# A list scheduler that books VectorE's and GpSimd's SBUF port as one resource, with matmul and ScalarE prices taken from a trace

## The chip, the core and the metric

The kernel runs on one core of one Trainium2 chip. The metric is the device time of one execution in microseconds. Five engines matter: TensorE (PE in the rows; its weight loads are PEld), VectorE (DVE), ScalarE (ACT), GpSimd (POOL) and SyncE (SP), which here only issues DMAs. Each engine works through its own instructions strictly in the order in which they were issued, and waits on semaphores where an operand or a buffer is not ready.

## What is computed

Two transformer stacks of two layers each follow one another on x, a float32 array of 512 tokens by 1024 features.

```python
def first_block(x, ...):
    for layer in range(2):
        x = x + 0.5 * rmsnorm(swiglu(rmsnorm(x, g[0]), gate, up, down), g[1])     # 1024 -> 2816 -> 1024
        x = x + rmsnorm(token_mixer(rmsnorm(x, g[2]), ...), g[3])                 # 16 heads, three kinds of attention
        x = x + 0.5 * rmsnorm(swiglu(rmsnorm(x, g[4]), gate, up, down), g[5])
    return x

def second_block(x, ...):
    for l in range(2):
        mix = concat(hgrn2_mixer(...), nsa_mixer(...)) @ w_out                    # a gated scan and sparse attention
        x = layer_norm(ALPHA * x + mix)
        x = layer_norm(ALPHA * x + (silu(x @ gate) * (x @ up)) @ down)
    return x
```

## The kernel before

Features lie on the 128 partitions and tokens along a partition, so x is eight tiles of 128x512 (in the rows `x_70`, `x_72`, and so on). Each projection is split in precision: a float32 weight block lands by DMA in a tile `raw`, and `weights` makes two tiles `ws` from it, hi = the block rounded to fp32r and lo = raw - hi. Activations are split in the same way into `h`, `m` or `gu`. `accum` then issues three fp32r matmuls for each block of 128 features (hi by hi, hi by lo, lo by hi) into a PSUM tile `mm`. So for 128x512 of weights there is one copy (VectorE or ScalarE) and one subtraction (VectorE or GpSimd), and TensorE gets twelve matmuls out of them.

Between the projections stand the norms. `rsqrt` is a chain of twelve tiny VectorE instructions on 128x2 tiles named `sm`: three `tensor_scalar`, then three rounds of one `tensor_tensor` and two `scalar_tensor_tensor`. `spread` transposes its result over the partitions (tile `nb`). `tail` and `post` scale the projected `y` by it (`tc<-y,nb`), add the product to x (`x<-x,tc`), and the next norm squares, adds (`tc<-tc`) and splits (`h<-tc,h`). Each half of 256 tokens goes through this by itself, so that TensorE can work on one half while the other is normed.

The order of all of this is not written by hand. A `Recorder` takes down every operation, with its operands, and `order` runs a list scheduler over them. `price` gives each operation a duration on each engine that may run it, `LAT` gives the delay to a consumer on another engine, and `attempt` runs forward in time: whenever an engine is idle it takes the ready operation of the smallest priority. The operations recorded with `nc.either` stand in the ready lists of two engines, and the one that is idle first takes them: copies and scalings go to VectorE or ScalarE, two-input operations (`tensor_tensor`) to VectorE or GpSimd. `holds` may keep an engine idle for something more urgent that comes soon. `backward` computes new priorities from the schedule found; twelve rounds are made and the shortest schedule by the prices is issued. `issue` (line 665) emits every instruction, so nearly all rows of the trace carry L665.

The prices that matter here, before: an fp32r matmul of n columns costs n/2.4 + 2.5 ns; ScalarE costs n/1.2 plus 52 or 94 ns; a GpSimd `tensor_tensor` 90 + 2.22 n ns; a VectorE `tensor_tensor` 70 + n/0.96 ns. VectorE and GpSimd are priced as independent of each other.

Of the kernel before, what the change touches and what calls it, by code (L numbers as in the profile page):

```python
# [26 lines left out]


class Buf:
    """A logical tile. Its slot and its Tile tile come when the order of instructions is known."""  # L30

    def __init__(self, parts, cols, dt, tag, name, dram=None):
        self.parts, self.cols, self.dt, self.tag, self.name, self.dram = parts, cols, dt, tag, name, dram
# [15 lines left out]


class V:
    """A view of a logical tile: partitions, and an access pattern over a partition's elements."""

    def __init__(self, buf, dt, p0, np_, off, dims, pstep=None, raw=None):
        self.buf, self.dt, self.p0, self.np, self.off, self.dims, self.raw = buf, dt, p0, np_, off, dims, raw
# [121 lines left out]

class Op:
    __slots__ = ("eng", "meth", "args", "kw", "outs", "ins", "deps", "users", "left", "cost", "lat", "tail", "ready",
                 "idx", "bufs", "func", "end", "start", "busy", "prices", "forms")  # L180

    def __init__(self, idx, eng, meth, args, kw):
        self.idx, self.eng, self.meth, self.args, self.kw = idx, eng, meth, args, kw
        vs = [x for x in args if isinstance(x, V)]
        outs = []
        ins = []
        for i, x in enumerate(args):
            if isinstance(x, V):
                (outs if i == 0 or i == 3 and meth == "pair" else ins).append(x)
        for k, x in kw.items():  # L190
            if isinstance(x, V):
                (outs if k == "accum_out" else ins).append(x)
        self.outs, self.ins = outs, ins
        self.deps, self.users = {}, []
        self.bufs = list({id(v.buf): v.buf for v in outs + ins}.values())
        self.func = args[2] if meth == "activation" and args[2] in SETS else None
        self.prices = {}
        self.forms = {}
        if meth == "copy":
            forms = {"vector": ("tensor_copy", args, kw), "scalar": ("activation", args + (AF.Copy,), kw)}  # L200
        elif meth == "scale":
            out, src, by = args
            forms = {"vector": ("tensor_scalar", (out, src, by, None), {"op0": OP.mult}),
                     "scalar": ("activation", (out, src, AF.Copy), {"scale": by})}
        else:
            forms = {e: (meth, args, kw) for e in (("vector", "gpsimd") if eng == "either" else (eng,))}
        for e in forms:
            self.eng = e
            self.meth, self.args, self.kw = forms[e]
            self.price()  # L210
            self.prices[e] = self.cost
        self.forms = forms
        self.choose(next(iter(forms)))

    def choose(self, eng):
        self.eng, self.cost = eng, self.prices[eng]
# [2 lines left out]
    def price(self):  # L219
        m = self.meth  # L220
        out = self.outs[0] if self.outs else None
        n = out.count() if out is not None else 0
        vs = self.ins + self.outs
        psum = any(v.buf.tag in PSUM for v in vs)
        if self.eng == "tensor":
            lhs = self.ins[0]
            load = lhs.count() / 1.2
            if lhs.dt == F32R:
                self.busy = n / 2.4
                self.cost = max(n / 2.4 + 2.5, load)  # L230
            elif m == "transpose":
                self.busy = self.cost = 107
            elif m == "pair":
                self.busy = 4 * n / 2.4
                self.cost = self.busy + 110
            else:
                self.busy = 4 * n / 2.4
                self.cost = max(self.busy + 2, 2 * load if n > 8 or n == 1 else load)
        elif self.eng == "sync":
            self.cost = max(475, vs[0].count() * vs[0].np / 90.0)  # L240
        elif self.eng == "scalar":
            self.cost = (52 if psum else 94) + n / 1.2 + (187 if "accum_out" in self.kw or isinstance(self.kw.get("bias"), V) else 0)
        elif self.eng == "gpsimd":
            self.cost = 90 + {"memset": 1.0, "tensor_copy": 3.5}.get(m, 2.22) * n
        else:
            ptr = any(v.count() == 1 for v in self.ins[1:])
            if m in ("tensor_copy", "tensor_scalar", "memset") and not psum:
                self.cost = 65 + n / 1.92 + (64 if ptr else 0)
            elif m == "reciprocal":
                self.cost = 65 + 8 * n / 0.96  # L250
            elif m == "tensor_tensor_reduce" or m == "tensor_reduce":
                self.cost = 75 + self.ins[0].count() / 0.96
            else:
                self.cost = 70 + n / 0.96 + (60 if psum and m == "scalar_tensor_tensor" else 0)
# [8 lines left out]
PSUM = ("mm", "at", "pv", "nb", "ah")  # L263
# [10 lines left out]


class Recorder:
    """Records instructions on logical tiles, orders them by a list scheduler, and issues them in that order."""

    def __init__(self, nc, tc, ctx, plan):
        self.bass_nc, self.tc, self.ctx, self.plan = nc, tc, ctx, plan  # L280
# [105 lines left out]
        return out  # L386

    def backward(self):
        """Schedules the reversed instructions, those that ended last first; the starts in forward time."""
        ops = self.ops  # L390
        engines = ("tensor", "scalar", "vector", "gpsimd", "sync")
        ready = {e: [] for e in engines}
        idle = {e: True for e in engines}
        left = [len(op.users) for op in ops]
        freed = [()] * len(ops)
        for b in self.bufs:
            if b.slot is not None and b.prior is not None and b.opener is not None:
                freed[b.opener] += tuple(b.prior.members)
                for i in b.prior.members:
                    left[i] += 1  # L400
        at = [0.0] * len(ops)
        late = [0.0] * len(ops)
        events = []
        for op in ops:
            if left[op.idx] == 0:
                heapq.heappush(ready[op.eng], (-op.end, op.idx))
        now, done = 0.0, 0
        while done < len(ops):
            for e in engines:
                if idle[e] and ready[e]:  # L410
                    i = heapq.heappop(ready[e])[1]
                    idle[e] = False
                    heapq.heappush(events, (now + ops[i].cost, 0, i))
            now, kind, i = heapq.heappop(events)
            op = ops[i]
            if kind:
                heapq.heappush(ready[op.eng], (-op.end, i))
                continue
            idle[op.eng] = True
            done += 1  # L420
            late[i] = -now
            for d in op.deps:
                left[d] -= 1
                at[d] = max(at[d], now + LAT[ops[d].eng][op.eng])
                if left[d] == 0:
                    heapq.heappush(events, (at[d], 1, d))
            for d in freed[i]:
                left[d] -= 1
                at[d] = max(at[d], now + (2000 if ops[d].eng == "sync" else 180))
                if left[d] == 0:  # L430
                    heapq.heappush(events, (at[d], 1, d))
        return late

    def attempt(self, prio):
# [20 lines left out]
        engines = ("tensor", "scalar", "vector", "gpsimd", "sync")  # L455
# [54 lines left out]
        def free_at(op, e):  # L510
            t = 0.0
            for b in op.bufs:
                if b.bank:
                    for g, end in b.last.items():
                        if g != e:
                            t = max(t, end + LAT[g][e])
            return t

        def holds(op, e, p):
# [5 lines left out]
                    return True  # L525
            return False

        def fits(op):
            return op.func is None or table in SETS[op.func]

        table = None
        now, done, total, out = 0.0, 0, len(ops), []
        loads = {}
        busy, window, cold = {}, 1, True
        while done < total:
            for e in engines:
                put_off = []
                while idle[e] and ready[e]:
                    op = None
                    while ready[e] and op is None:  # L540
                        p, i = heapq.heappop(ready[e])
                        if ops[i].start is not None:
                            continue
                        t = free_at(ops[i], e)
                        if t > now:
                            push(t, "ready", ops[i])
                            continue
                        if e == "scalar" and not fits(ops[i]):
# [8 lines left out]
                                    break  # L557
                            if op is not None:
                                break
                        if e in HOLD and holds(ops[i], e, p):  # L560
                            put_off.append((p, i))
                            op = None
                            break
# [22 lines left out]
                    if not fits(op):  # L586
                        cost += 1300
                        table = SETS[op.func][0]
                        loads[op.idx] = table
                    op.start, op.end = now, now + cost  # L590
                    for b in op.bufs:
                        if b.bank:
                            b.last[e] = op.end
# [75 lines left out]

SET_SLACK = 4000  # L670
HOLD = ('gpsimd', 'scalar', 'vector')
HOLD_A = 0.3
HOLD_B = 0.5
ROUNDS = 12
# [1179 lines left out]
```

## Time and profile before

| | |
|---|---|
| time, median of 3 runs | 3787.7 us (3786.96 to 3789.73) |
| span of the profiled execution, first to last instruction | 3776.2 us |
| TensorE busy | 3631.1 us (96%) |
| VectorE busy | 2241.1 us (59%) |
| ScalarE busy | 1699.6 us (45%) |
| GpSimd busy | 1078.0 us (29%) |
| mean granted TensorE clock | 0.978 of 2.4 GHz |

The profiled execution is told by its span alone; the timed runs lie 10.8 to 13.5 us above it, which is what stands before the first and behind the last instruction. Busy times are the union of an engine's instructions. An engine that waits on another engine's port inside an instruction counts as busy.

### The profile page before, as it was taken

How to read it: one execution, taken by the hardware profiler on the slowest of the kernel's cores; microseconds unless marked ns; L12 is line 12 of the kernel's file. 1: busy time of each engine (PE TensorE's matmuls, PEld its weight loads, DVE VectorE, ACT ScalarE, POOL GpSimd, SP SyncE). 2: the span in 40 equal slices, each digit the busy share in tenths (PEclk: the TensorE clock that was granted, in tenths of full speed). 3: DMA queues.
4: the chain of work that ended last, by engine and by line, in shares of the span. 5: the costliest groups of instructions: out<-in, count | busy, mean ns of one | idle time of the engine just before them, and what ended most of it. 6: DMA issues, size and time to landing. Idle time of an engine off the chain costs nothing.

```text
span 3776.2 us, 56593 instructions
## 1 busy us (share of the span) xinstructions
PE 3631.1 (96%) x20836; PEld 3016.9 (80%) x20836; DVE 2241.1 (59%) x4611; ACT 1699.6 (45%) x3550; POOL 1078.0 (29%) x999
## 2 busy tenths in 40 slices
PE   8999899999999999899899999999999999999998
PEld 7878877778898889767788897668888977678888
DVE  7443787764367545886844384677333766674335
ACT  5333456543344334565433354465332555654324
POOL 3220422443224211522633042334111333232112
PEclk9999999999999999999999999899999999999999
DMA  5224422232353224312322452013323531123234
GB/s 165 95 93 133 157 81 76 96 112 95 95 150 124 95 92 144 130 59 74 125 98 93 118 173 93 29 32 123 112 95 102 172 98 51 40 90 129 95 90 139
DMA packets 121622, 393.08 MB, mean 104 GB/s; under 512 B 14813, under 2 KB 20102, under 8 KB 121345
## 3 DMA queue, kind: packets, MB, share of 16 engines
q1 hardware_dynamic: 121344, 389.47, 32.6%
q8 instruction: 164, 2.69, 0.3%
q14 instruction: 114, 0.93, 0.1%
HBM read 384.65 MB, written 4.77 MB: 103 GB/s over the span
## 4 chain that ended last, share of the span: by engine, by line
PE 47%; DVE 6%; issue 1%; ACT 1%; POOL 0%; DMA 0%; ACTq 0%; DVEq 0%; POOLq 0%; SPq 0%
PE mm L665 38%; PE at L665 4%; PE ah L665 2%; PE pv L662 2%; DVE ws L665 1%; PE ah L662 1%; DVE sm L665 1%; DVE tc L665 1%; DVE hw L665 1%; DVE h L665 1%; DVE x L665 0%; PE nb L665 0%; ACT ws L665 0%; POOL ws L665 0%; ACT L659 0%
## 5 line engine op out<-in xcount | busy, mean ns | idle before, releaser
L665 PE MATMUL mm<-h,ws 128*128 128x512 f32 (+1 forms) x9792 | 2102.3, 362 | 53.9 <-DVE ws L665 16.9
L665 PEld LDWEIGHTS mm<-h,ws 128*128 128x128 f32 x9792 | 1645.8, 192 | 357.8 <-issue 25.1
L665 ACT ACTIVATE ws<-raw 128x512 fp32r<-128x512 f32 (+1 forms) x1283 | 782.0, 616 | 1417.8 <-PE mm L665 1370.8
L665 POOL TENSOR_TENSOR ws<-raw,ws 128x512 fp32r<-128x512 f32 (+1 forms) x506 | 654.5, 1295 | 2061.6 <-ACT ws L665 1592.3
L665 DVE TENSOR_TENSOR ws<-raw,ws 128x512 fp32r<-128x512 f32 (+2 forms) x926 | 682.3, 741 | 798.6 <-ACT ws L665 732.1
L665 PE MATMUL mm<-gu,ws 128*128 128x256 f32 (+1 forms) x4752 | 813.0, 323 | 11.9 <-DVE ws L665 7.3
L665 PEld LDWEIGHTS mm<-gu,ws 128*128 128x128 f32 x4752 | 692.2, 191 | 90.5 <-DVE ws L665 12.9
L665 DVE TENSOR_TENSOR te<-te,mm 128x256 f32<-128x256 f32 (+1 forms) x228 | 98.8, 460 | 279.9 <-PE mm L665 275.2
L665 PE MATMUL mm<-ws,h 128*128 128x256 f32 (+1 forms) x1344 | 254.9, 303 | 1.7 <-DVE sm L665 0.7
L665 PE MATMUL mm<-m,ws 128*128 128x256 f32 (+1 forms) x1248 | 218.3, 321 | 7.5 <-DVE ws L665 7.2
L665 PEld LDWEIGHTS mm<-ws,h 128*128 128x128 f32 x1344 | 203.2, 195 | 14.7 <-issue 6.3
L665 PEld LDWEIGHTS mm<-m,ws 128*128 128x128 f32 x1248 | 175.6, 195 | 32.3 <-issue 12.4
L665 ACT ACTIVATE row<-row,sm 128x512 f32<-128x512 f32 (+2 forms) x267 | 148.3, 572 | 58.2 <-DVE sm L665 57.2
L665 ACT ACTIVATE gu<-te 128x256 fp32r<-128x256 f32 (+1 forms) x210 | 89.5, 452 | 129.8 <-DVE te L665 118.4
L665 DVE TENSOR_TENSOR te<-te,rt 128x256 f32<-128x256 f32 x157 | 119.4, 792 | 0.5
L665 DVE CAST ws<-raw 128x512 fp32r<-128x512 f32 x149 | 97.7, 656 | 33.2 <-PE mm L665 27.7
L665 DVE TENSOR_TENSOR te<-mm,rt 128x256 f32<-128x256 f32 x176 | 67.8, 419 | 81.7 <-PE mm L665 80.4
L665 POOL TENSOR_TENSOR hw<-hw 128x256 f32<-128x256 f32 x106 | 88.7, 846 | 92.9 <-ACT hw L665 80.0
L665 PE MATMUL at<-c_ident,row 128*128 128x128 f32 x528 | 114.4, 286 | 0.4 <-DVE sm L665 0.3
L665 DVE TENSOR_TENSOR gu<-te,gu 128x256 fp32r<-128x256 f32 (+1 forms) x159 | 94.2, 611 | 30.3 <-ACT gu L665 26.0
L665 DVE CUSTOM_DVE_ANT_0 row<-at,T 128x128 f32<-128x128 f32 (+1 forms) x180 | 88.8, 509 | 25.6 <-PE at L665 23.6
L665 ACT ACTIVATE hw<-hw 128x256 f32<-128x256 f32 (+2 forms) x181 | 75.5, 456 | 55.1 <-DVE hw L665 28.1
(249 smaller groups left out, 3429.7 us busy)
## 6 DMA issues: line engine op xcount, KB each, us to landing
raw<-in_wg_dram SPq DMA_DIRECT2D x156, 512.0 KB, 3.3
raw<-in_wu_dram SPq DMA_DIRECT2D x156, 512.0 KB, 3.2
raw<-in_wd_dram SPq DMA_DIRECT2D x144, 512.0 KB, 3.5
raw<-in_wd_dram SPq DMA_DIRECT2D x72, 384.0 KB, 3.2
raw<-in_wout_dram SPq DMA_DIRECT2D x52, 512.0 KB, 3.3
raw<-in_w_f_dram SPq DMA_DIRECT2D x52, 512.0 KB, 3.4
raw<-in_win_f_dram SPq DMA_DIRECT2D x44, 512.0 KB, 3.3
raw<-in_win_v_dram SPq DMA_DIRECT2D x20, 512.0 KB, 3.2
```

The source lines that it names most:

```text
L662: nc.tensor.matmul(*args[0:3], **kw)
L665: r = getattr(getattr(nc, op.eng), op.meth)(*args, **kw)
```

## The change

`port` (new) marks, for each engine, the operations that use the shared port: on GpSimd all that read a tile from SBUF, on VectorE those with two inputs of more than one element in SBUF, and copies or `tensor_scalar` from SBUF to SBUF. In `attempt`, such an operation cannot start on one of the two engines while the other holds the port (`held`). `late` (new) lets GpSimd take a two-input operation only when VectorE is busy and would finish it later, counting what is ready ahead of it on VectorE. Three prices change.

```diff
+        self.ports = {e: self.port(e) for e in forms}
...
+    def port(self, e):
+
+        wide = [v for v in self.ins if v.count() > 1]
+        if e == "gpsimd":
+            return bool(wide)
+        if e != "vector":
+            return False
+        near = [v for v in wide if v.buf.tag not in PSUM]
+        if len(near) == 2:
+            return True
+        return (len(near) == len(wide) == 1 and self.outs[0].buf.tag not in PSUM
+                and self.forms[e][0] in ("tensor_copy", "tensor_scalar"))
...
-                self.cost = max(n / 2.4 + 2.5, load)
+                self.cost = max(n / 2.4 + 13, load)
...
-            self.cost = (52 if psum else 94) + n / 1.2 + (187 if "accum_out" in self.kw or isinstance(self.kw.get("bias"), V) else 0)
+            self.cost = (62 if psum else 106) + n / 1.2 + (187 if "accum_out" in self.kw or isinstance(self.kw.get("bias"), V) else 0)
...
-            self.cost = 90 + {"memset": 1.0, "tensor_copy": 3.5}.get(m, 2.22) * n
+            self.cost = 130 + {"memset": 1.0, "tensor_copy": 3.5}.get(m, 2.2) * n
...
+        def late(op):
+            if idle["vector"]:
+                return False
+            t = until["vector"]
+            n = sum(ops[x[1]].prices["vector"] for x in ready["vector"] if ops[x[1]].start is None and x[0] < prio[op.idx])
+            return t + n + op.prices["vector"] > now + op.prices["gpsimd"] * POOL_W
...
+                        if ops[i].ports[e]:
+                            t = max(t, held["vector" if e == "gpsimd" else "gpsimd"])
                         if t > now:
                             push(t, "ready", ops[i])
                             continue
...
+                        if e == "gpsimd" and "vector" in ops[i].prices and not late(ops[i]):
+                            put_off.append((p, i))
+                            op = None
+                            break
...
+                    until[e] = op.end
+                    if op.ports[e]:
+                        held[e] = op.end
...
+POOL_W = 1.0
```

The operations recorded are the same in both kernels; which engine issues them and in what order is not. In the built programs GpSimd's `tensor_tensor` instructions go from 961 to 253 (of those with 512 elements from 506 to 149), and VectorE's from 2711 to 3419: 708 of them move. VectorE's copies, casts and `tensor_scalar` go from 835 to 692, and ScalarE's activations from 3274 to 3417: 143 of them move.

Two places show it, both at the end of the first layer's attention block, where its norm and the start of the second feed-forward block stand close together. First GpSimd's order there. Before, from the splits of the gate weights (`ws<-raw,ws`) over the additions to x to the splits of the next `h`:

```order
L665 TENSOR_TENSOR ws<-raw,ws 128x512 x5
L665 TENSOR_TENSOR te<-te,rt 128x256
L665 TENSOR_TENSOR gu<-te,gu 128x256
L665 TENSOR_TENSOR x_72<-x_72,tc 128x256
L665 TENSOR_TENSOR x_74<-x_74,tc 128x256
L665 TENSOR_TENSOR x_78<-x_78,tc 128x256
L665 TENSOR_TENSOR ws<-raw,ws 128x512
L665 TENSOR_TENSOR x_88<-x_88,tc 128x256
L665 TENSOR_TENSOR ws<-raw,ws 128x512
L665 TENSOR_TENSOR h<-tc,h 128x256
L665 TENSOR_TENSOR ws<-raw,ws 128x512
L665 TENSOR_TENSOR h<-tc,h 128x256
```

And GpSimd's whole order over the same place now, from the splits of the attention output `m` to an addition to x of the next norm:

```order
L697 TENSOR_TENSOR m<-y,m 128x512 x4
L697 TENSOR_TENSOR ws<-raw,ws 128x512 x4
L697 TENSOR_TENSOR x_84<-x_84,tc 128x256
L697 TENSOR_TENSOR ws<-raw,ws 128x512 x2
L697 TENSOR_TENSOR te<-te,rt 128x256
L697 TENSOR_TENSOR ws<-raw,ws 128x512 x2
L697 TENSOR_TENSOR ws<-raw,ws 128x256
L697 TENSOR_TENSOR x_72<-x_72,tc 128x256
```

Of the four additions to x, the two splits of `h` and all but a few of the weight splits nothing is left on GpSimd here. They stand on VectorE, whose order at the norm of the second half of the tokens was this, from the end of the `rsqrt` chain:

```order
L665 SCALAR_TENSOR_TENSOR sm<-sm 128x2
L665 TENSOR_TENSOR te<-te,mm 128x256
L665 TENSOR_TENSOR ws<-raw,ws 128x512
L665 TENSOR_TENSOR tc<-y,nb 128x256 x2
L665 TENSOR_TENSOR x_70<-x_70,tc 128x256
L665 TENSOR_TENSOR tc<-y,nb 128x256 x4
L665 TENSOR_TENSOR x_76<-x_76,tc 128x256
L665 TENSOR_TENSOR x_84<-x_84,tc 128x256
L665 TENSOR_TENSOR tc<-y,nb 128x256 x2
L665 TENSOR_SCALAR tc<-x_72,c_gains 128x256
L665 TENSOR_TENSOR x_94<-x_94,tc 128x256
```

and is this now:

```order
L697 SCALAR_TENSOR_TENSOR sm<-sm 128x2 x2
L697 TENSOR_TENSOR ws<-raw,ws 128x512
L697 CAST ws<-raw 128x512
L697 TENSOR_TENSOR tc<-y,nb 128x256 x4
L697 TENSOR_TENSOR x_70<-x_70,tc 128x256
L697 TENSOR_TENSOR x_72<-x_72,tc 128x256
L697 TENSOR_TENSOR x_74<-x_74,tc 128x256
L697 TENSOR_TENSOR x_84<-x_84,tc 128x256
L697 TENSOR_TENSOR tc<-y,nb 128x256 x2
L697 TENSOR_TENSOR x_78<-x_78,tc 128x256
L697 TENSOR_TENSOR tc<-y,nb 128x256
L697 TENSOR_TENSOR x_76<-x_76,tc 128x256
```

Before, VectorE made four of the eight additions to x and GpSimd the other four; now all eight stand on VectorE (the last two a few rows on).

## Rows read from the trace of the kernel before

**Rows 1.** Page: busy us, share, instructions; VectorE's busy tenths in 40 slices.

```profile
PE 3631.1 (96%) x20836; PEld 3016.9 (80%) x20836; DVE 2241.1 (59%) x4611; ACT 1699.6 (45%) x3550; POOL 1078.0 (29%) x999
...
DVE  7443787764367545886844384677333766674335
```

**Rows 2.** Span and mean granted TensorE clock.

```profile
core 0: 3776.2 us, clock 0.978
```

**Rows 3.** Windows: length; busy us (count) of PE, PEld, DVE, ACT, POOL; clock; DMA.

```profile
300.00:400.00 100.00, 100.00 (x571) 83.02 (x570) 33.03 (x54) 37.29 (x71) 3.42 (x4) 0.98 0.52 156
400.00:500.00 100.00, 85.46 (x635) 80.23 (x634) 90.57 (x192) 50.53 (x114) 50.68 (x46) 0.97 0.44 142
700.00:800.00 100.00, 84.63 (x606) 80.32 (x605) 84.86 (x172) 49.97 (x105) 55.69 (x51) 0.91 0.39 126
...
800.00:1000.00 200.00, 199.21 (x863) 161.76 (x863) 89.56 (x159) 72.18 (x141) 63.54 (x53) 1.00 0.29 95
```

**Rows 4.** TensorE's waits: total us, times, longest.

```profile
PE mm L665 <- DVE ws L665: 31.3, 35, 5.2
PE nb L665 <- DVE sm L665: 27.9, 17, 3.8
PE mm L665 <- ACT ws L665: 16.6, 5, 12.0
PE mm L665 <- POOL ws L665: 8.0, 11, 1.5
PE nb L665 <- DVE tc L665: 6.7, 10, 1.6
PE mm L665 <- DVE te L665: 5.7, 5, 3.8
PE nb L665 <- POOL tc L665: 5.0, 4, 2.8
```

**Rows 5.** Timeline around 741 us: start, length, instruction.

```profile
740.92 1.28 POOL L665 TENSOR_TENSOR ws<-raw,ws 128x512 fp32r<-128x512 f32 x1 [2.68 <-ACT ws L665]
740.93 1.29 DVE L665 TENSOR_TENSOR sm<-sm 128x2 f32<-128x2 f32 x1
```

**Rows 6.** VectorE's groups, 300 to 400 us: busy us, mean ns, idle before.

```profile
L665 DVE TENSOR_TENSOR ws<-raw,ws 128x512 fp32r<-128x512 f32 x36 | 24.8, 692 | 53.9 <-ACT ws L665 50.7 <-PE mm L665 3.0
...
L665 DVE CAST ws<-raw 128x512 fp32r<-128x512 f32 x1 | 0.4, 428 | 3.4 <-PE mm L665 3.4
L665 DVE TENSOR_SCALAR sm<-sm 128x2 int32<-128x2 int32 x2 | 0.3, 170 | 0.1
L665 DVE TENSOR_TENSOR sm<-sm 128x2 f32<-128x2 f32 x1 | 0.2, 161 | 0.0
```

**Rows 7.** VectorE's groups, 700 to 800 us.

```profile
L665 DVE TENSOR_TENSOR ws<-raw,ws 128x512 fp32r<-128x512 f32 x23 | 20.1, 882 | 5.7 <-ACT ws L665 3.0 <-PE mm L665 2.7
L665 DVE TENSOR_TENSOR h<-tc,h 128x256 fp32r<-128x256 f32 x13 | 8.2, 642 | 0.1
L665 DVE TENSOR_TENSOR x<-x,tc 128x256 f32<-128x256 f32 x10 | 7.9, 816 | 0.0
L665 DVE TENSOR_TENSOR tc<-tc 128x256 f32<-128x256 f32 x9 | 6.6, 731 | 0.2
...
L665 DVE TENSOR_TENSOR sm<-sm 128x2 f32<-128x2 f32 x12 | 5.0, 415 | 0.3
L665 DVE TENSOR_SCALAR sm<-sm 128x2 int32<-128x2 int32 x8 | 4.9, 618 | 0.2
L665 DVE SCALAR_TENSOR_TENSOR sm<-sm 128x2 f32<-128x2 f32 x24 | 4.9, 205 | 0.7
...
L665 DVE TENSOR_TENSOR te<-te,mm 128x256 f32<-128x256 f32 x8 | 3.3, 417 | 2.7 <-PE mm L665 2.7
```

**Rows 8.** GpSimd's largest group, 700 to 800 us.

```profile
L665 POOL TENSOR_TENSOR ws<-raw,ws 128x512 fp32r<-128x512 f32 x26 | 34.5, 1329 | 27.3 <-ACT ws L665 22.6 <-PE mm L665 3.0 <-issue 0.8
```

**Rows 9.** A VectorE group with one input in PSUM, whole span.

```profile
L665 DVE TENSOR_TENSOR te<-te,mm 128x512 f32<-128x512 f32 x36 | 24.8, 688 | 92.8 <-PE mm L665 92.8
```

More of the change, by code (lines that the diff above doesn't have):

```diff
@@ L179 @@
     __slots__ = ("eng", "meth", "args", "kw", "outs", "ins", "deps", "users", "left", "cost", "lat", "tail", "ready",
-                 "idx", "bufs", "func", "end", "start", "busy", "prices", "forms")
+                 "idx", "bufs", "func", "end", "start", "busy", "prices", "forms", "ports")
     def __init__(self, idx, eng, meth, args, kw):
@@ L531, in attempt @@
         table = None
+        held = {"vector": 0.0, "gpsimd": 0.0}
+        until = dict.fromkeys(engines, 0.0)
         now, done, total, out = 0.0, 0, len(ops), []
```

## Prediction, made before the changed kernel was run

> **What bounds the kernel now.** I read the busy times first. TensorE is busy 3631.1 of 3776.2 us, VectorE 59% and GpSimd 29% [rows 1, 2]. TensorE's idle time is so 3776.2 - 3631.1 = 145 us. Its granted clock averages 0.978; the clock has two levels, 1.2 and 2.4 GHz, so the low level costs at most 0.022 x 3776 = 83 us of full-speed work [rows 2]. Then the windows, which tell where this happens. Between 800 and 1000 us TensorE works through 863 matmuls of 512 columns in 200 us and waits for nothing: 231.7 ns for one, at a granted clock of 1.00. Between 700 and 800 us, where a norm closes the attention block and the next feed-forward block starts, it is busy 84.6 of 100 us at a clock of 0.91, while VectorE is busy 84.9 and GpSimd 55.7; 400 to 500 us looks alike (90.6 and 50.7) [rows 3]. So the kernel is bound by TensorE in the long projections and by VectorE with GpSimd in the stretches around the norms. TensorE's own waits say the same: the largest are for `ws` and the `rsqrt` chain `sm`, both from VectorE, and 8.0 + 5.0 = 13.0 us are for GpSimd [rows 4].
>
> **What the port does in this trace.** A `tensor_tensor` on 128x2 that takes 161 ns where GpSimd is nearly idle [rows 6] took 1.29 us when it started 10 ns behind a GpSimd instruction of 1.28 us [rows 5]: it was held for the whole of it. From the means of 700 to 800 us against undisturbed ones (692 ns for `ws`, 161 and 170 ns for `sm`; 417 ns for 128x256, from `te<-te,mm`, which has an input in PSUM) [rows 6, 7], the time held is: `ws` 23 x (882 - 692) = 4.4 us, `h` 13 x 225 = 2.9, `x` 10 x 399 = 4.0, `tc<-tc` 9 x 314 = 2.8, `sm` 12 x 254 + 8 x 448 = 6.6; together 20.7 us beside 55.7 us of GpSimd's work [rows 3], or 0.37 us for each. Over GpSimd's 1078 us [rows 1] that makes some 400 us of VectorE's 2241, an estimate.
>
> **The change part by part.** *708 `tensor_tensor` move from GpSimd to VectorE.* 357 have 512 elements, the others mostly 256: 357 x 0.692 + 351 x 0.417 = 393 us of new VectorE work. GpSimd keeps 253 of 961, so if the held time falls with its count, 400 x 708 / 961 = 295 us come back. *143 copies and scalings move to ScalarE*, which relieves VectorE of 143 x 0.43 = 61 us at most [rows 6]; I take 55, since many have 256 elements. Sum for VectorE: 2241 + 393 - 295 - 55 = 2284 us. For 700 to 800 us: 51 GpSimd instructions, 26 of them `ws` [rows 3, 8]; 74% of them cost 19 x 0.692 + 19 x 0.417 = 21 us, 20.7 x 0.74 = 15 us come back and about 2 us of copies leave, so 84.9 becomes 89 us. **In throughput the move is a wash, slightly against the change.** What is left is latency, and the plan.
>
> *Latency of GpSimd's share.* A `ws` comes after 692 instead of 1329 ns [rows 6, 8]. TensorE's 13.0 us of waits for GpSimd should about halve: -6 us. *Latency of the `rsqrt` chain.* Of its 14.8 us in rows 7 (three `sm` groups) 6.6 are held time, 45%. TensorE waits 27.9 us for it [rows 4]; 27.9 x 0.45 x 0.74 = -9 us. *Other waits for VectorE* (31.3 + 6.7 + 5.7 [rows 4]): a VectorE that is 5% fuller delays them by 5%, +2 us. *ScalarE* gets 143 of 1699.6 us' worth of instructions more, about 4%; its 16.6 us of TensorE's waits [rows 1, 4] grow by 1 us. *Clock.* TensorE's idle time falls by 12 of 145 us, 8%, and with it, I assume, the share at the low level: 83 x 0.08 = -7 us.
>
> *The prices and the new order.* All 20,836 matmuls stand in another order, and no row of before prices that. The matmul's price of 512 columns goes from 215.8 to 226.3 ns where the row shows 231.7 [rows 3], so the plan now counts on a slower TensorE, nearer to what it does. What a nearer plan can give lies between nothing gained and a loss of the size of the waits that the order itself causes. Upwards I bound it by half of the seven waits shown (half of 101 us) plus the clock in proportion (50 x 83/145 = 29): -80 us. Downwards by an order whose waits grow by a fifth, 20 us. I take -16, near the small end, because the waits shown are of a few us after a chain of data, which an order can only fill with other work, not shorten.
>
> The Trainium skill, "TensorE: Matmul & The Clock Gate", section "Back-to-back issue gap", gives the distance of warm matmuls as N/2.4 GHz plus about 2.5 ns, which is the price before. The trace disagrees: 231.7 ns against 215.8 for 512 columns. By that rule the new price is an error, the order term is its upper bound of +20 instead of -16, and the sum +1 us, 3789; the rows leave that 0.04, which is held in rival 2.
>
> Sum: -6 - 9 + 2 + 1 - 7 - 16 = -35 us. The span of 3776.2 us would be 3741; the median of the timed runs lies 11.5 us above the span, and I keep that: 3787.7 - 35 = **3752 us**. Less than 0.2% (7.6 us) can't be told from no change with this kernel.
>
> **The rivals.** *1. VectorE becomes the bound at the norms (slower).* GpSimd's work beside a VectorE instruction with an input in PSUM was free: `te<-te,mm` of 512 elements shows 688 ns in the mean of 36, no longer than an undisturbed one [rows 6, 9]. This free overlap is given up. The point that decides is how much held time comes back: if only half of the 15 us does, VectorE needs 84.9 + 21 - 7.5 - 2 = 96 of 100 us between 700 and 800, and by the same ratio over 100 between 400 and 500. Added VectorE work then lies on the path: 11 us for each such stretch. Five of the 40 slices of the span show VectorE at eight tenths or more [rows 1]; half of 11 us on each, and the low clock that goes with idle time (83/145 of it), give 5 x 5.5 x 1.57 = +43 us, less the 15 us of latency gained: 3816 us. Against it: 74% fewer instructions that can hold the port, each booked against VectorE, should give back more than half. The Trainium skill, "SBUF — State Buffer", section "Who interferes with whom", says that a VectorE instruction with at most one SBUF input outside its two-port modes does not contend with GpSimd. The trace agrees: 688 ns [rows 9]. By that rule this overlap was indeed free before, and what is left of it on GpSimd is now decided by who would end sooner alone.
>
> *2. No change.* The two engines did the same work through one port before and do it after; 2284 against 2241 us is the same. Then only the latency terms are left and the order takes them back: -15 + 8 = 3781 us, or within 0.2%. For it speaks that TensorE is busy 96% [rows 1]. The Trainium skill, "Trace Analysis", section "Optimizing Scalar/DVE Operations", says that shifting work between GpSimd and VectorE might not help since they share a port; by that rule the shift back need not help either, which is this case.
>
> *3. Much faster.* The plan was wrong by far (engines thought independent, TensorE 7% too fast by 215.8 to 231.7), and an order made with right prices removes half of the waits and of the low clock: -80 us from the order instead of -16, 3688 us.
>
> *4. The change doesn't do what it says:* GpSimd's remaining instructions still overlap with VectorE's, because nothing on the chip enforces the plan. That is inside rival 1 (held time doesn't come back) and needs no chance of its own.
>
> **How the numbers follow.** My forecast (3710 to 3775) gets 0.42, rival 3 (below 3710) 0.18, rival 2 (3775 to 3795) 0.18, rival 1 (above 3795) 0.22. The predicted time is the forecast's. The range to leave out no more than 2 in 10: from 3695, which leaves out the far half of rival 3 (0.08), to 3815, which leaves out the far half of rival 1 (0.11), 0.19 in all. The forecast and rival 3 alone reach from 3688 to 3775. Faster by over 0.2% means below 3780: 0.42 + 0.18 and a little of rival 2, 0.62. Slower, above 3795: 0.22 and a little of rival 2, 0.24. Between: 0.14.
>
> **What would show it.** Right: mean durations of VectorE's `sm`, `x<-x,tc` and `h<-tc,h` at 700 to 800 us fall towards 161, 417 and 417 ns; GpSimd's busy time is near 300 us and VectorE's within 80 us of 2284; TensorE's waits for `sm` and for GpSimd fall by a third or more; the mean clock rises from 0.978. The latency step is wrong if the durations fall and the waits don't. The throughput step is wrong if VectorE's busy time goes over 2400 us, with idle time of TensorE before `ws` from VectorE above 31.3 us. The order term is wrong if stretches without any wait of before, 800 to 1000 us for one, get longer, or if TensorE's idle time falls by far more than 30 us. The whole is wrong if TensorE's busy time itself grows by tens of us at an equal clock.

## The result and the profile after

| | before | after |
|---|---|---|
| median of 4 runs each | 3787.3 us (3786.67 to 3789.73) | 3675.1 us (3665.83 to 3678.68) |
| ratio | | 0.9699 [0.9684, 0.9714] |

The kernel is 112 us faster. The forecast of 3752 us had the sign and missed the size by a factor of three, and the time lies below the range. The profiled execution after took 3672.3 us, 1.8 us above its span. So the 10.8 to 13.5 us by which the timed runs before lie above the profiled span are mostly a difference between executions, not time before the first and behind the last instruction; the two spans differ by 106 us, the medians by 112.

The page of the kernel after, busy us, share and instructions of each engine, then VectorE's busy tenths in 40 slices, answers to [rows 1]; its span and granted clock to [rows 2]:

```profile
PE 3592.3 (98%) x20836; PEld 2990.6 (81%) x20836; DVE 2205.6 (60%) x5176; ACT 1750.3 (48%) x3690; POOL 289.4 (8%) x291
...
DVE  6443788755366545986844385677333767774336
```

```profile
core 0: 3670.5 us, clock 0.985
```

GpSimd lost 789 us of busy time and VectorE, which took over its work, lost 36 as well. TensorE's idle time went from 145.1 to 3670.5 - 3592.3 = 78.2 us, which is 67 us; the other 39 of the 106 us that the span lost are TensorE's own busy time, at the same number of matmuls and a clock of 0.985 instead of 0.978.

Three stretches of after in windows, with the columns of [rows 3]. Work ends earlier now, so 680 to 780 us holds what 700 to 800 us held:

```profile
300.00:400.00 100.00, 100.00 (x571) 81.84 (x571) 33.87 (x60) 38.23 (x71) 1.49 (x2) 1.00 0.54 159
...
680.00:780.00 100.00, 89.58 (x647) 84.73 (x646) 78.64 (x208) 56.47 (x126) 7.08 (x6) 0.95 0.41 138
800.00:1000.00 200.00, 200.00 (x866) 162.17 (x865) 90.95 (x197) 69.73 (x134) 3.33 (x3) 1.00 0.29 95
```

The long projections are as they were (866 instead of 863 matmuls in 200 us). At the norm VectorE does more instructions (208 instead of 172) in less time (78.6 instead of 84.9 us), TensorE is busy 89.6 instead of 84.6, and the clock rose from 0.91 to 0.95. Why VectorE got faster stands in its groups of 680 to 780 us, which answer to [rows 7] (busy us, mean ns of one, idle before):

```profile
L697 DVE TENSOR_TENSOR ws<-raw,ws 128x512 fp32r<-128x512 f32 x48 | 32.2, 686 | 5.1 <-ACT ws L697 4.2 <-PE mm L697 0.6
L697 DVE TENSOR_TENSOR x<-x,tc 128x256 f32<-128x256 f32 x15 | 7.7, 555 | 0.0
L697 DVE TENSOR_TENSOR h<-tc,h 128x256 fp32r<-128x256 f32 x16 | 6.9, 450 | 0.2 <-ACT h L697 0.2
...
L697 DVE SCALAR_TENSOR_TENSOR sm<-sm 128x2 f32<-128x2 f32 x24 | 3.8, 160 | 0.7
L697 DVE TENSOR_TENSOR te<-te,mm 128x256 f32<-128x256 f32 x8 | 3.3, 418 | 5.4 <-PE mm L697 5.4
L697 DVE TENSOR_TENSOR sm<-sm 128x2 f32<-128x2 f32 x12 | 1.9, 161 | 0.4
L697 DVE TENSOR_SCALAR sm<-sm 128x2 int32<-128x2 int32 x8 | 1.3, 169 | 0.2
```

`ws` fell from 882 to 686 ns, the three `sm` groups from 415, 618 and 205 to 161, 169 and 160 ns: the first three of these four at their undisturbed values of [rows 6], the last at the 158 ns that it takes in experiment 3, where GpSimd is silent. `x<-x,tc` is at 555 ns, still above the 417 that it takes there. `te<-te,mm`, with an input in PSUM, is at 418 ns where it was at 417.

TensorE's largest waits after, against [rows 4] (total us, times, longest):

```profile
PE mm L697 <- DVE ws L697: 17.6, 17, 5.0
PE nb L697 <- DVE tc L697: 16.9, 8, 11.6
PE mm L697 <- ACT ws L697: 10.1, 9, 4.0
PE nb L697 <- DVE sm L697: 6.4, 6, 2.4
...
PE mm L697 <- POOL ws L697: 0.8, 2, 0.5
```

The wait for the `rsqrt` chain fell from 27.9 to 6.4 us, that for `ws` from VectorE from 31.3 to 17.6, those for GpSimd nearly to nothing. One wait grew: for VectorE's `tc`, 6.7 to 16.9 us, 11.6 of it in one place.

### The profile page after: what moved, and what is told of

The parts are those of the page before. It is cut to its first block, busy times and chain, and to the rows that moved or that the text cites. A ratio compares the mean times of both kernels' runs of the same rounds, so it can differ in the third digit from the quotient of the medians.

```text
span 3670.5 us, 56063 instructions
## 1 busy us (share of the span) xinstructions
PE 3592.3 (98%) x20836; PEld 2990.6 (81%) x20836; DVE 2205.6 (60%) x5176; ACT 1750.3 (48%) x3690; POOL 289.4 (8%) x291
## 4 chain that ended last, share of the span: by engine, by line
PE 92%; DVE 5%; ACT 1%; issue 1%; DMA 1%; SPq 0%; POOL 0%; ACTq 0%; DVEq 0%
PE mm L697 78%; PE at L697 6%; PE pv L694 2%; PE ah L697 2%; PE nb L697 2%; PE ah L694 1%; DVE tc L697 1%; DVE ws L697 1%; DVE x L697 1%; DVE sm L697 1%; DVE h L697 0%; ACT tc L697 0%; DMA cw<-in_cw_dram 0%; SPq L697 0%; ACT ws L697 0%
## 5 line engine op out<-in xcount | busy, mean ns | idle before, releaser
L697 ACT ACTIVATE ws<-raw 128x512 fp32r<-128x512 f32 (+2 forms) x1355 | 822.8, 616 | 1365.5 <-PE mm L697 1329.8
L697 DVE TENSOR_TENSOR ws<-raw,ws 128x512 fp32r<-128x512 f32 (+1 forms) x1286 | 880.5, 690 | 780.7 <-ACT ws L697 662.4
L697 POOL TENSOR_TENSOR ws<-raw,ws 128x512 fp32r<-128x512 f32 (+1 forms) x146 | 184.6, 1265 | 2338.5 <-PE mm L697 1206.2
L697 ACT ACTIVATE gu<-te 128x256 fp32r<-128x256 f32 (+1 forms) x226 | 100.4, 452 | 141.6 <-DVE te L697 140.4
L697 DVE TENSOR_TENSOR gu<-te,gu 128x256 fp32r<-128x256 f32 (+1 forms) x228 | 104.0, 463 | 14.5 <-ACT gu L697 2.5
L697 PE MATMUL at<-NK,NQ 128*128 128x256 f32 (+5 forms) x256 | 89.1, 395 | 0.9 <-DVE sm L697 0.9
L697 PEld LDWEIGHTS at<-c_ident,row 128*128 128x128 f32 x528 | 67.9, 142 | 19.5 <-issue 6.0
L697 DVE TENSOR_TENSOR te<-te,rt 128x256 f32<-128x256 f32 x174 | 83.5, 490 | 0.0
```

The source lines that it names most:

```text
L697: r = getattr(getattr(nc, op.eng), op.meth)(*args, **kw)
```

## The experiments

**Theory A, the held port:** GpSimd's instructions stop VectorE's, and fewer of them mean shorter chains at the norms; this acts in any order. **Theory B, the plan:** what counts is that the planner's numbers became truer (rival 3's mechanism), the new matmul price above all. A third reading lies between: GpSimd's own results were late, since it is slow, and holding VectorE mattered little. Every kernel was timed in three rounds beside the kernel before, whose median was 3783 to 3788 us on these chips. "Held" below is my own sum over VectorE's groups: their time, less their count at the means that the same groups have in `e3_old_order_no_pool`, where GpSimd is silent. By it 389 us were held before and 71 after.

**1. The prices alone** (`e1_prices_only`), in the kernel before:

```diff
-                self.cost = max(n / 2.4 + 2.5, load)
+                self.cost = max(n / 2.4 + 13, load)
```

with the two other prices of the change.

> The kernel before with only the three new prices (matmul, ScalarE, GpSimd); no port, no late rule. Theory A (GpSimd held VectorE's instructions, and that delay was what TensorE waited for): the engines keep their shares, GpSimd stays near 1078 us busy and some 400 us of VectorE's time stays held, so 3780 us, give or take 10. Theory B (the plan counted on a TensorE 7% too fast, and the order made with the right price brings the gain): most of the 112 us, 3700 to 3730 us.

Measured: 3785.8 us, ratio 1.0008 [0.9997, 1.0018]; held 407 us. No change.

**2. The port and the `late` rule with the three old prices** (`e2_port_only`).

> The changed kernel with the three old prices: port and late rule alone. Theory A: nearly the whole gain, 3675 to 3700 us, GpSimd under 350 us busy. Theory B: little, 3755 to 3785 us.

Measured: 3662.5 us, 0.9677 [0.9663, 0.9692]; held 52 us. The whole gain is there without the prices.

**3. The order of before, GpSimd's work on VectorE** (`e3_old_order_no_pool`). In `issue`, each two-input operation that the plan gave to GpSimd, 961 in all, is issued at its place on VectorE:

```diff
+                if op.eng == "gpsimd" and "vector" in op.prices:
+                    op.choose("vector")
```

> The order of the kernel before, untouched on every engine, except that each two-input operation that GpSimd had is issued on VectorE at the same place in the order. No held time can be left. Theory A in its strong form (held time and GpSimd's slower instructions cost the time, whatever the order): 3690 to 3720 us. Theory B, or A in a weak form in which a plan is needed that knows VectorE's load: VectorE gets 393 us more work and loses 400 us of held time in an order not made for it, 3760 to 3830 us.

Measured: 3717.2 us, 0.9827 [0.9813, 0.9842]. Its page and TensorE's waits:

```profile
PE 3608.1 (97%) x20836; PEld 2994.1 (81%) x20836; DVE 2281.3 (61%) x5572; ACT 1702.9 (46%) x3550; POOL 11.1 (0%) x38
```

```profile
PE mm L667 <- DVE ws L667: 24.6, 32, 4.7
PE mm L667 <- ACT ws L667: 14.1, 4, 11.3
PE nb L667 <- DVE sm L667: 11.1, 17, 2.4
PE nb L667 <- DVE tc L667: 7.6, 13, 2.5
```

Not one matmul stands elsewhere and VectorE has 961 instructions more, yet its busy time grew only from 2241 to 2281 us and the kernel gained 66 us. The wait for `sm` has the same 17 places as in [rows 4], and fell from 27.9 to 11.1 us.

**4. The order of after, GpSimd's old work on GpSimd** (`e4_new_order_old_pool`). The 961 operations of before are issued on GpSimd again (`OLD_POOL` is their list):

```diff
+                if op.meth == "tensor_tensor" and "gpsimd" in op.prices:
+                    op.choose("gpsimd" if op.idx in OLD_POOL else "vector")
```

> The order of the changed kernel on TensorE and ScalarE, but the 961 two-input operations that GpSimd had before are issued on GpSimd again, at the same place in the order. Theory A: held time is back near 400 us and nearly all of the gain is lost, 3760 us or more. Theory B: the order keeps most of it, 3700 to 3725 us.

Measured: 3758.6 us, 0.9931 [0.9911, 0.9950]; held 292 us. Of the 112 us only some 26 are left, as theory A has it, though less than 400 us is held. Its two largest waits show what else comes back when an order that does not plan for it uses GpSimd:

```profile
PE nb L699 <- POOL tc L699: 26.4, 15, 12.4
PE mm L699 <- POOL ws L699: 22.5, 37, 2.5
```

These two make 48.9 us, and TensorE's idle time is 3760.4 - 3630.0 = 130.4 us, 52 more than after. So in this order most of the idle time that came back is the third reading, GpSimd's own results being late, while the wait for `sm` grew only from 6.4 to 15.2 us. The loss speaks against theory B, but it doesn't show holding to be its cause.

**5 to 7. The two rules apart, and no GpSimd.** All three have the old prices. In `e5_late_only` nothing books the port, in `e6_port_without_late` the test of `late` is gone, and `e7_no_pool` plans with VectorE alone:

```diff
-                        if ops[i].ports[e]:
+                        if False:
...
-                        if e == "gpsimd" and "vector" in ops[i].prices and not late(ops[i]):
+                        if False:
...
-            forms = {e: (meth, args, kw) for e in (("vector", "gpsimd") if eng == "either" else (eng,))}
+            forms = {e: (meth, args, kw) for e in (("vector",) if eng == "either" else (eng,))}
```

> The late rule alone, with the three old prices: GpSimd takes only what VectorE would finish later, the port is not booked. Theory A1 (it is enough that GpSimd does little, the booking adds nothing): GpSimd under 400 us busy and 3660 to 3685 us. Theory A2 (the plan must know when the port is held): GpSimd's instructions still fall on VectorE's, 3690 to 3730 us.

> The booked port alone, with the three old prices, without the late rule: an idle GpSimd takes any two-input operation when the port is free. Theory A1: GpSimd keeps much of its work and holds the port for 1.3 us where VectorE would need 0.7; 3720 to 3790 us. Theory A2: the booking is what counts, 3660 to 3700 us.

> Two-input operations are recorded for VectorE alone, so that the scheduler plans without GpSimd (the three old prices). Theory A1: GpSimd's remaining share is worth nothing, 3655 to 3675 us, level with the port alone. Theory A2: the share that fits beside VectorE's instructions with an input in PSUM is worth something, 3685 to 3720 us, no better than the old order without GpSimd (3717).

| | us | ratio | GpSimd busy | held |
|---|---|---|---|---|
| `e5_late_only` | 3700.5 | 0.9776 [0.9759, 0.9794] | 710.0 | 255 |
| `e6_port_without_late` | 3879.5 | 1.0240 [1.0221, 1.0258] | 1461.8 | 101 |
| `e7_no_pool` | 3672.6 | 0.9702 [0.9687, 0.9716] | 10.8 | 0 |

Without GpSimd the kernel is as fast as after: what GpSimd keeps there is worth nothing that this can tell. The `late` rule by itself brings 85 us, and more with the port booked. The port booked without `late` is the one of the three that loses, and more than either theory had foreseen. Its page, TensorE's waits, VectorE's wait for GpSimd's `tc`, and its `sm` groups over the whole span:

```profile
PE 3646.0 (94%) x20836; PEld 3031.3 (78%) x20836; DVE 1679.0 (43%) x3924; ACT 1779.2 (46%) x3727; POOL 1461.8 (38%) x1509
```

```profile
PE nb L697 <- DVE sm L697: 83.3, 18, 7.1
PE mm L697 <- POOL ws L697: 28.6, 41, 3.7
```

```profile
DVE tc L697 <- POOL tc L697: 84.8, 7, 17.2
```

```profile
L697 DVE SCALAR_TENSOR_TENSOR sm<-sm 128x2 f32<-128x2 f32 x192 | 51.2, 267 | 6.0
L697 DVE TENSOR_SCALAR sm<-sm 128x2 int32<-128x2 int32 x64 | 36.1, 564 | 1.6
L697 DVE TENSOR_TENSOR sm<-sm 128x2 f32<-128x2 f32 x96 | 33.5, 349 | 3.2
```

When either engine may take the port, the one that is idle takes it: GpSimd gets 1509 instructions and VectorE falls to 1679.0 us. A weight split takes 1329 ns on GpSimd and 692 on VectorE [rows 6, 8], and TensorE's wait for `sm` is three times what it was. Only 101 us are held here, but 64 of them in the `sm` instructions (120.8 us against 57.0 in experiment 3; 39 were held there before). VectorE also waits 84.8 us, in seven places, for `tc` from GpSimd. So the place of the held time counts as well as its sum; how the loss divides between the held chain and GpSimd's late `tc` was not tested.

**8 and 9. Which of GpSimd's work mattered.** As experiment 3, for the operations with `op.outs[0].buf.tag == "ws"` alone (506 weight splits), and for the 455 others alone.

> The order of the kernel before on every engine, with only the weight splits (506 of GpSimd's 961 two-input operations) issued on VectorE at their place; the 455 of the norms, gates and scans stay on GpSimd. If held time counts as such, it goes by GpSimd's time: the splits are 655 of 1078 us busy, so 61% of the 66 us, 3743 us. If what counts is only the work around the norms standing on GpSimd, under 20 us of the gain, 3765 us or more. If the splits' holding alone is what TensorE feels, over 50 us of the gain, 3735 us or less.

> The complement of the run with the splits moved: in the order of the kernel before, the 455 other two-input operations of GpSimd (norms, gates, scans, gated units) are issued on VectorE at their place, the 506 weight splits stay on GpSimd. If the two parts add up to the 66 us of both together, 56 being the splits' part, this gives 10 us, 3773 us. If each part by itself removes the same waits, 25 us or more, 3755 us or less. If it overloads VectorE while the splits still hold it, 3785 us or more.

Measured: 3728.9 us, 0.9848 [0.9828, 0.9869], and 3764.5 us, 0.9942 [0.9927, 0.9958]. The weight splits bring 1.5%, the others 0.6%; both together 1.7%, so the two overlap, by a little more than the intervals. TensorE's wait for `sm`, first with the splits on VectorE, then with only the others there:

```profile
PE nb L667 <- DVE sm L667: 11.8, 17, 2.4
```

```profile
PE nb L667 <- DVE sm L667: 31.0, 19, 3.5
```

So it is the weight splits that held the `rsqrt` chain: without them its wait falls as in experiment 3 (11.1 us) and 3 us of the chain are held, with them 39 are held, as before. The second time lies between the forecasts of 3773 and 3755 us.

**10. The tuning of `late`** (`e10_port_w13`), with the old prices; GpSimd's price counts 1.3 times in its comparison.

> Port and late rule with the old prices, POOL_W 1.3 instead of 1.0: GpSimd takes an operation only if VectorE would finish it later by more than 0.3 of GpSimd's duration, so less often. If GpSimd's last share still costs, 3650 to 3660 us; if it is worth something, towards the run without GpSimd, 3665 to 3675 us.

```diff
-POOL_W = 1.0
+POOL_W = 1.3
```

Measured: 3683.4 us, 0.9732 [0.9715, 0.9748]; no gain, outside both forecasts, and 21 us above `e2_port_only`.

**11. The matmul price as a knob.** The kernel after with + 12, + 14 and + 18 ns for its + 13 (`e15_matmul_12`, `e11_matmul_14`, `e16_matmul_18`), and `e7_no_pool` with the new prices (`e12_no_pool_new_prices`).

> The changed kernel with the matmul price at n/2.4 + 14 instead of + 13 ns, 0.4% of a matmul: nothing that should matter, so it measures how far the time scatters with the order alone. If the 12 us between the changed kernel and the one with old prices is scatter, this lies anywhere from 3655 to 3690 us; if prices act smoothly, 3675 us within 3 us.

> Planned without GpSimd, with the three new prices instead of the old ones. If the new prices cost time by themselves, again 10 to 15 us more than with the old (3672), 3682 to 3688 us. If they bring a better order, under 3668 us. If it is scatter, within 10 us either way, of either sign.

> The changed kernel with the matmul price at n/2.4 + 12 instead of + 13 ns: a second measure of the scatter by the order alone, beside + 14 (3657) and + 13 (3675). Scatter: anywhere from 3650 to 3690 us. A smooth price: 3680 to 3695 us, as + 14 was 18 us faster.

> The changed kernel with the matmul price at n/2.4 + 18 ns, which is 231.3 ns for 512 columns and so the measured 231.7. If the plan gains by a truer price, 3650 us or less; if it is scatter, anywhere from 3650 to 3690 us.

| price of a matmul | us | ratio |
|---|---|---|
| + 12 | 3662.4 | 0.9667 [0.9652, 0.9681] |
| + 13 (the kernel after) | 3675.1 | 0.9699 [0.9684, 0.9714] |
| + 14 | 3656.8 | 0.9659 [0.9645, 0.9674] |
| + 18 | 3675.0 | 0.9697 [0.9682, 0.9711] |
| no GpSimd, + 13 | 3663.0 | 0.9678 [0.9663, 0.9692] |

One nanosecond of a price, under half a per cent of a matmul, moves the time by 13 to 18 us, up or down, and the truest price (231.7 ns is + 18) is not the best. So differences of up to some 18 us between versions that plan anew can't be put down to a rule: `e2_port_only`, after, `e7_no_pool` and `e12_no_pool_new_prices` are one result. + 14 is the fastest kernel that was run, 18 us below after, by such scatter and for no reason that was shown.

**12. GpSimd holds the port and does nothing else.** The kernel of experiment 3, in which GpSimd also makes 506 subtractions that nobody uses, where it split weights before, into a scratch tile of its own; 440 columns (`e13_idle_holds`; 35 of the 506 blocks have only 256), or 8 (`e14_idle_touch`):

```diff
+                if twin:
...
+                    w = min(440, op.outs[0].count())
+                    nc.gpsimd.tensor_tensor(scratch[:, :w], op.args[1][:, :w].real(), op.args[2][:, :w].real(), op=OP.subtract)
```

> The old order with everything on VectorE (3717 us), plus 506 GpSimd subtractions that nobody needs: wherever GpSimd had split a weight block, it again reads raw and hi, up to 440 columns, and writes the difference to a scratch tile. Results come from VectorE as before, so only the port and the release of the ws buffer are touched. If holding the port is what costs: 200 us or more of VectorE's time held again and most of the 66 us lost, 3760 us or more. If it was the lateness of GpSimd's own results (1329 against 692 ns): 3715 to 3735 us.

> The same with GpSimd subtracting only 8 columns: the same 506 instructions, waits and buffer releases, but each over in a tenth of the time. By the holding theory 3717 us again, within 10. If the added instructions or the release of the buffers cost, the same loss as with 440 columns.

Measured: 3926.4 us, 1.0363 [1.0348, 1.0379], and 3727.0 us, 0.9844 [0.9820, 0.9868]. The page, two VectorE groups over the whole span and TensorE's waits, with 440 columns:

```profile
PE 3695.6 (94%) x20836; PEld 3042.4 (77%) x20836; DVE 2621.5 (67%) x5572; ACT 1702.5 (43%) x3550; POOL 671.3 (17%) x544
```

```profile
L670 DVE TENSOR_TENSOR ws<-raw,ws 128x512 fp32r<-128x512 f32 x1344 | 1122.5, 838 | 727.0 <-ACT ws L670 647.1 <-PE mm L670 65.2 <-ACT V L670 1.9
...
L670 DVE TENSOR_TENSOR te<-te,mm 128x512 f32<-128x512 f32 x36 | 24.8, 688 | 91.3 <-PE mm L670 91.3
```

```profile
PE mm L670 <- DVE ws L670: 58.6, 67, 4.0
PE nb L670 <- DVE sm L670: 43.0, 21, 3.6
PE nb L670 <- DVE tc L670: 20.5, 21, 2.5
```

The same group of VectorE with 8 columns, and in experiment 3:

```profile
L670 DVE TENSOR_TENSOR ws<-raw,ws 128x512 fp32r<-128x512 f32 x1344 | 924.4, 691 | 798.7 <-ACT ws L670 722.9 <-PE mm L670 61.2 <-ACT V L670 1.8
```

```profile
L667 DVE TENSOR_TENSOR ws<-raw,ws 128x512 fp32r<-128x512 f32 x1344 | 920.2, 688 | 791.2 <-ACT ws L667 712.2 <-PE mm L667 66.4 <-PE nb L667 0.6
```

The long subtractions cost 199 us more than the short ones (3926.4 - 3727.0) in the same number and at the same places, and the short ones hardly more than none (3717.2). One of 8 columns took 419 ns, a third of the long one's time and not the tenth that was expected. What changed is VectorE: 343 us held instead of 8. Their results go nowhere, so the third reading can't explain this loss; its share in the kernel before is bounded below. Their one other effect is that the `raw` and `ws` tiles that they read come free later. The wait of SyncE's queue, with 440 columns (total us, times, longest), shows it:

```profile
SPq L670 <- POOL scratch L675: 79.2, 80, 3.4
```

No other computing engine waits for `scratch`, and what SyncE's queue waits reaches nobody: the longest wait of a computing engine for a transfer is 3.6 us, once, for the input x, and it is 3.4 us without the subtractions. So holding by itself slows the kernel.

## Why the prediction was wrong, step by step

**What is shown.** In the old order the cause is GpSimd's work, and holding by itself slows the kernel as theory A has it (experiments 3 and 12); B's mechanism, truer prices, gave nothing (experiments 1 and 11). The third reading has a share: of the 38.8 us of TensorE's idle time that experiment 3 took away, 13.0 were waits for GpSimd's own results, a third. The 112 us are 66 us of GpSimd's work being on VectorE in the old order (experiment 3), and some 45 us of an order planned for that (3717.2 against 3672.6 in experiment 7, with a scatter of up to 18). The forecast had -19 us for the first part (-6 - 9 + 2 + 1 - 7) and -16 for the second.

**The steps that failed: the latency terms, all too small.** "TensorE waits 27.9 us for it; 27.9 x 0.45 x 0.74 = -9 us" takes a wait to shrink in the proportion in which the chain behind it shrinks. In the same order the wait fell by 16.8 us (the formula without its 0.74 gives 12.6), and after by 21.5. A wait is what a chain reaches beyond the work that covers it, so what is taken from the chain can come off the wait whole. Over the whole span the 352 `sm` instructions took 96.4 us before and 57.0 in experiment 3: 39 us lost, more than there was to wait. The other waits for VectorE, which I let grow by +2 us with its busy time, shrank: `ws`, `tc` and `te` together from 43.7 to 37.5 us in experiment 3 (`te` 5.3). GpSimd's 13.0 us went wholly, not by 6: in experiment 3 because all 961 operations leave it, and after 0.8 us for `ws` and 0.7 for `h` are left, with 253 still on it. ScalarE's `ws` wait fell by 2.5 us in experiment 3, where its work is unchanged, and after by 6.5 instead of growing by 1. In experiment 3 these four make -38.5 us, about what TensorE's idle time lost there (145.1 to 3714.4 - 3608.1 = 106.3); the forecast had -12.

**"In throughput the move is a wash"** was nearly right and led astray. VectorE's busy time is 2205.6 us, within 80 of 2284; held time was estimated at 400 us and came to 389; 295 us were to come back, and 318 did. In experiment 3 VectorE is even busier than before, and the kernel is faster. Equal busy time is not equal cost: a piece of GpSimd's work can stop a tiny instruction of the `rsqrt` chain as well as a large one [rows 5]. In experiment 12 343 us of held time cost 209 us against experiment 3, 0.6 for each; by that rate, an estimate that takes it over from a kernel whose VectorE is fuller, the 389 us of before were worth some 240, of which VectorE's added work took some 170 back.

**The clock** went the way that was forecast, by a proportion that the runs don't bear out. I took the cost of the low level to fall with TensorE's idle time. By the mean clocks it fell from 83 to 0.015 x 3670.5 = 55 us, so by 28 where the term has 7; TensorE's idle time fell by 67 of 145 us, which in proportion would give 38. In experiment 3, with 28 us more idle time than after, the clock is the same 0.985; in experiment 7, with 47 us less than before, it is only 0.981. The other 11 of the 39 us of busy time that TensorE lost are not the clock's.

**The order term** of -16 was under-sized and argued from the wrong rule. I let it rest on the matmul price; the prices moved nothing. The prediction's own sign against this term came: TensorE's idle time fell by 67 us, far more than 30. What goes with the gain is a plan that gives this work to VectorE, be it by `late` and the port or by leaving GpSimd out (experiment 7). Experiment 4 shows the other side: with GpSimd's old share in that order TensorE waits 26.4 us for `tc` from it. Nor did such an order mainly shorten the waits that the profile lists. From experiment 3 to 7 the span lost 43.3 us, of which TensorE's idle time is 8.5 (106.3 to 97.8) and its busy time 34.8 (3608.1 to 3573.3), at a lower clock. The distances between starts show short stalls that went: of the matmuls of 256 or 512 columns into `mm`, which undisturbed follow one another within 0.35 us, 103 are followed by the next one 0.5 to 1.2 us after their start in experiment 3, 75 us together, and 28 in experiment 7, 18 us together. A record of such a matmul is itself 0.28 to 0.42 us long, so part of such a stall counts as busy. By the formula in the Trainium skill, "TensorE: Matmul & The Clock Gate", section "Back-to-back issue gap", the new price would have been an error. For that the prediction held +20 us; with either price the time is the same within scatter.

**The rivals.** Rival 1 (VectorE becomes the bound) did not come: VectorE between 680 and 780 us is at 78.6 us, below before's 84.9. Its mechanism exists the other way round: in experiment 12 held time pushes VectorE's results late. The wait for VectorE's `tc`, which grew from 6.7 to 16.9 us (27.6 in experiment 7), may be the part of it that came. Rival 2 rested on equal busy times and falls with that. The Trainium skill, "Trace Analysis", section "Optimizing Scalar/DVE Operations", says that shifting work between the two may not help; the runs show that it can help by 66 us in an unchanged order. Rival 3 gave the size (3688), in part by luck: experiment 1 refutes its right prices, while its other half, a plan that thought the engines independent, fits the 45 us of the order. Rival 4 did not come as such, since 71 of 389 us are still held; but GpSimd had also become less busy. For each us of its work 0.36 us were held before (389 of 1078), 0.25 after (71 of 289), 0.36 with `late` alone (255 of 710) and 0.07 with the port booked alone (101 of 1462). So bookings come true in part, and most of the held time went with the work itself.

**What stays open.** Why the planned orders have fewer short stalls, and how the 45 us of the plan divide between the port's booking and `late`: `e5_late_only` (3700.5) and `e2_port_only` (3662.5) differ by more than the scatter, but each is one order.

## What to carry to other kernels

Where two engines share a port, count part of a slow engine's time (here 0.36 us of each) as time held on the fast one, and try the plain alternative first: the same order with that work issued on the fast engine. When a chain gets shorter, bound what its wait can lose by the whole of the shortening, up to the whole wait, and not by the wait's share in proportion. Before a rule in a list scheduler gets credit, change one price by half a per cent, and take the differences that this makes as the measure of no change.

## What was not expected of the hardware

GpSimd's 506 subtractions of up to 440 columns, 1.34 us in the mean for 128x440 and used by nobody, raised VectorE's `ws` subtractions to 838 ns in the mean of 1344, from 688 without them; those of 8 columns, 419 ns in the mean (506 in 212.2 us), left them at 691. The short ones held VectorE for 8.1 us in all, 16 ns each, the long ones for 343, 0.68 us each. So GpSimd's busy time alone does not say how long it holds VectorE: a third of the time on it gave a fortieth of the holding. VectorE's `te<-te,mm` of 512 elements, with an input in PSUM, took 687 to 689 ns in the mean in every one of these kernels. The Trainium skill, "SBUF — State Buffer", section "Who interferes with whom", says that a VectorE instruction with at most one SBUF input, outside its two-port modes, does not contend with GpSimd. The trace agrees: before, all 36 ran beside a `tensor_tensor` of GpSimd, 688 ns in the mean and none above 691, and they took 687 with GpSimd silent (experiment 3).
